# Loading the stacks of the RWKV chains in fourteen paced pieces instead of two bursts

## The chip, the cores and the metric

The kernel runs on one core of one Trainium2 chip. The metric is the device time of one launch in microseconds (us): the time before is the median of three runs. Beside those runs there is one profiled execution, from which every view of the profile is taken.

## The reference, cut to what matters

Two trunk layers work on 1024 latent and 256 context tokens of 1024 channels. Layer 0 mixes tokens with a bidirectional RWKV-7 recurrence, layer 1 with attention; both are followed by an MLP. The change lies inside the recurrence of layer 0, which for each of 16 heads of 64 channels, and for each of two directions, is

```
def _wkv_step(state, inp):
    r, w, k, v, kk, bvec = inp
    sa = jnp.einsum('bhvk,bhk->bhv', state, -kk)
    state = state * w[:, :, None, :] + sa[..., None] * bvec[:, :, None, :] + v[..., None] * k[:, :, None, :]
    y = jnp.einsum('bhvk,bhk->bhv', state, r)
    return state, y
```

`_rwkv_scans` runs it forward and backward, first over the context tokens (from a zero state) and then over the latent tokens (from the context's last state), and adds the two outputs.

## The kernel before

The recurrence is done in chunks of 32 tokens: 8 context chunks and 32 latent chunks, so 40 steps in a row. Per chunk the work is turned into small matrix products. An earlier stage (`Prep`) computes the operands and writes them to three DRAM tensors: `S["ST"]` (for every chunk the stationary operands of the first and last product, called the stack, and in its ninth slot the inverted triangular matrices), `S["LS"]` (the stationary operands of the state update) and `S["V"]` (the values).

The stage of the chains (`Chain`, `staggered`) then walks the 40 steps. Two neighbouring chunks form a granule; there are 20 granules, and the list `Chain.seq` gives their order. The 16 heads with their two directions are packed into four pairs (0 to 3); pairs 0 and 1 share one stack tile (`lp` 0), pairs 2 and 3 another (`lp` 1). One pair's step has four pieces of work, each with 16 small matrix products on TensorE:

- `ps_x` (L848): stack times the state and values in tile `SV`; ScalarE copies it to `X` (L850).
- `ps_x` (L854): the masked inverse `T` times `X`; the results are copied back into `SV` (L861). `T` for the next step is made by GpSimd (L830) from the ninth slot of the stack.
- `ps_s` (L868): `LS` times `SV`, the new state; VectorE scales it into the `SV` of the next step (L872).
- `ps_y` (L877): the second half of the stack times `SV`, the output, copied or added to `y` (L880, L882).

`staggered` counts ticks t: a step takes 16 ticks, a granule 32, and pair l does its four pieces at ticks 4l + 0, 5, 10 and 11 of each step. So four ticks hold one piece of each kind, of four different pairs, and TensorE always has other pairs' products between two dependent ones. The readout of finished blocks (`early`, `middle`) is woven between the ticks and runs mostly on VectorE and GpSimd.

The operands of granule i + 1 are loaded while granule i runs. The stack tiles have two buffers (pool `gp`), as have the `LS` and `SV` tiles, so a load of granule i + 1 waits until the readers of granule i - 1 are through. All loads are issued by SyncE, whose DMA queue (SP) works in order. `Chain.run` calls `load` at the start of pair 1's granule (tick 4, for `lp` 0) and of pair 3's granule (tick 12, for `lp` 1). One call issues the whole stack (1152 KB, L805), two `LS` transfers of 256 KB (L808) and, for `lp` 1, eight `SV` transfers of 64 KB (L811): 14 transfers and 3840 KB per granule, each waiting for its buffer only. The first granule's loads are issued ahead of the stage (`issue_after`).

The instructions are put on their engines by a scheduler that keeps the order of data; a hand-made dependency between two instructions can be added with `add_manual_dep`.

Of the kernel before, what the change touches and what calls it, by code (L numbers as in the profile page):

```python
# [9 lines left out]
F32 = mybir.dt.float32  # L10
# [19 lines left out]
QUAD = {(0, 0): 3, (0, 1): 1, (1, 0): 2, (1, 1): 0}  # L30
# [172 lines left out]
def drain(*gens):  # L203
    for g in gens:
        for _ in g:
            pass


def weave(main, n, *tracks):


    state = [[0, *t, *(0, n)[len(t) - 2:]] for t in tracks]
    for i, _ in enumerate(main):
        for t in state:
            while i >= t[3] and t[0] < t[1] * (i + 1 - t[3]) / (t[4] - t[3]):
                t[0] += 1
                next(t[2], None)
    drain(*(t[2] for t in state))


def _chain(gens):
    for g in gens:
        yield from g
# [551 lines left out]
class Lanes:  # L775
# [21 lines left out]
                nc.scalar.copy(t[rows, h].rearrange("p l d a e c -> p (l d a) e c"), eye)  # L797
        self.ST = {}

    def load(self, k, lp, i):  # L800

        nc, S = k.nc, k.S
        ST, LS, SV = self.gp.tile([128, 2, 9, 2, 64], F32, name="ST", tag=f"ST{lp}"), self.LS[lp][i % 2], self.SV[i % 2]
        self.ST[lp, i] = ST
        nc.sync.dma_start(out=ST.rearrange("p l u c e -> p (l u c e)"), in_=S["ST"][:, lp, i].rearrange("p l u c e -> p (l u c e)"))  # L805
        for h in range(2):
            anti = slice(64 - h * 64, 128 - h * 64)
            nc.sync.dma_start(out=LS[anti, h].rearrange("p l d a e c -> p (l d a e c)"), in_=S["LS"][h, i, :, :, lp * 2:lp * 2 + 2].rearrange("b s l d a f e -> (b s) (l d a f e)"))  # L808
        for a, h, d in itertools.product(range(2), range(2), range(2) if lp == 1 else ()):
            q = (QUAD[a, h] ^ 1) * 32  # L810
            nc.sync.dma_start(out=SV[q:q + 32, h, a, 2 * d:2 * d + 2].rearrange("p c l e -> p (c l e)"), in_=S["V"][a, h, :, Chain.seq[i][d]].rearrange("s c l e -> s (c l e)"))  # L811


class Chain:
# [17 lines left out]
    def step(self, s):  # L832
        k, nc, pr, L = self.k, self.k.nc, self.pr, self.L
        i, c = divmod(s, 2)
        both = lambda c: slice(c, 4 - c, 3 - 2 * c)
        gf, gb = self.seq[i]
        rev, lp, ln = gf > gb, pr // 2, pr % 2
        ST, ls, SV = L.ST[lp, i], L.LS[lp][i % 2], L.SV[i % 2]
        stack = lambda ct2, h, d, o: ST[:, ln, h * 4 + ct2 * 2 + d, c, o:o + 32]
        sv = lambda h, ct2, d: SV[:, h, ct2, 2 * d + (c ^ d), pr, :]  # L840
        units = [(ct2, h, d) for d in range(2) for ct2 in range(2) for h in range(2)]
        if s == 0:
            self.inverses(0)
        T = self.T
        xu = L.px.tile([128, 2, 2, 64], F32, name="ps_x", tag="xu")
        for ct2, h, d in units:
            q = QUAD[ct2, h] * 32
            nc.tensor.matmul(xu[q:q + 32, 0, d, :], stack(ct2, h, d, 0), sv(h, ct2, d), start=True, stop=True, tile_position=(0, q))  # L848
        X = L.xp.tile([128, 2, 64], F32, name="X", tag=f"X{pr}")
        L.copied = nc.scalar.copy(X, xu[:, 0])  # L850
        yield
        for ct2, h, d in units:
            q = QUAD[ct2, h] * 32
            nc.tensor.matmul(xu[q:q + 32, 1, d, :], T[:, d, q // 32, :], X[:, d, :], start=True, stop=True, tile_position=(0, q))  # L854
        lo, hi = sorted((2 * gf + c, 2 * gb + 1 - c))
        first = lo not in self.seen
        self.seen |= {lo, hi}
        for ct2 in range(2):
            for h in range(2):
                q = QUAD[ct2, h] * 32  # L860
                (nc.vector.tensor_copy if first and ct2 == h == 0 else nc.scalar.copy)(SV[q:q + 32, h, ct2, both(c), pr, :], xu[q:q + 32, 1])  # L861
        yield
        if s + 1 < self.n:
            self.inverses(s + 1)
            i2, c2 = divmod(s + 1, 2)
            pst = L.pss.tile([128, 2, 2, 64], F32, name="ps_s", tag="s")
            for ct2, h, d in units:
                nc.tensor.matmul(pst[h * 64:h * 64 + 64, ct2, d, :], ls[:, h, ln, d, ct2, :, c], sv(h, ct2, d), start=True, stop=True, tile_position=(0, h * 64))  # L868
            for h in range(2):
                rows = slice(h * 64, h * 64 + 64)  # L870
                pt = k.c["PT"][rows, pr * 2:pr * 2 + 2, :, s + 1].unsqueeze(3).to_broadcast([64, 2, 2, 64])
                nc.vector.tensor_tensor(L.SV[i2 % 2][rows, h, :, both(c2), pr, :], pst[rows], pt, ALU.mult)  # L872
        yield
        psy = L.py.tile([128, 2, 64], F32, name="ps_y", tag="y")
        for ct2, h, d in units:
            q = QUAD[ct2, h] * 32
            L.last = nc.tensor.matmul(psy[q:q + 32, d ^ rev, :], stack(ct2, h, d, 32), sv(h, ct2, d), start=True, stop=True, tile_position=(0, q))  # L877
        o = self.y[:, lo:hi + 1:hi - lo, :]
        if first:
            nc.scalar.copy(o, psy)  # L880
        else:
            nc.vector.tensor_tensor(o, o, psy, ALU.add)  # L882

    def run(self):
        for s in range(self.n):
            if self.pr % 2 and s % 2 == 0 and s // 2 + 1 < len(self.seq):
                self.L.load(self.k, self.pr // 2, s // 2 + 1)
            yield from self.step(s)
            yield

# [10 lines left out]


STAGES = (0, 5, 10, 11)


def staggered(gens):


    for t in range(16 * Chain.n + 16):
        for l, g in enumerate(gens):  # L910
            if t >= 4 * l and (t - 4 * l) % 16 in STAGES:
                next(g, None)
        yield


# [90 lines left out]
def phase_ab(k, xstack):  # L1006


    tc, nc, S = k.tc, k.nc, k.S
    with ExitStack() as es:  # L1010
# [4 lines left out]
        ips, rs, ws, ls, hs, ps = (ExitStack() for _ in range(6))  # L1015
# [17 lines left out]
        y = [yp.tile([128, 40, 64], F32, name=f"y{p}", tag=f"y{p}") for p in range(4)]  # L1033
        ro = [Readout(k, p, y[p], rn) for p in range(4)]

        def early():

            k.cload("lnq", pool=rn)
            k.tables = nc.scalar.preload_act_table_set("natural_log_exp_and_others")
            k.order(k.tables, L.copied)  # L1040
            yield from _chain([r.gates() for r in ro])
            for r in ro:
                yield from r.center(4, False)
                yield from r.scale(4, False)

        with ExitStack() as cs:
            L = Lanes(k, cs)
            with tc.issue_after(k.late.ins):
                for lp in range(2):
                    L.load(k, lp, 0)  # L1050
            middle = _chain([_chain([r.center(b, False), r.scale(b, False)]) for b in (1, 2) for r in ro])
            weave(staggered([Chain(k, L, p, y[p]).run() for p in range(4)]), 16 * Chain.n + 16, (4 * 4 + 4 * 7, early(), 16 * 5, 16 * 31), (8 * 7, middle, 16 * 33))
        ips.close()
        rs.close()
        xs = parts(xstack.enter_context(tc.tile_pool(name="xs", reuse_waits="tile", bufs=1, side="right")), range(KT))
# [35 lines left out]
        if k.dbg and "o" in k.O:  # L1091
            for ct in range(KT):
                for t0, n in TB:
                    t = tmp.tile([128, 512], F32, name="o_db", tag="ro_z")
# [353 lines left out]
def build(tc, I, O, dbg=None):  # L1448
    with ExitStack() as ctx:
        k = K(tc, I, O, ctx, dbg)  # L1450
        setup(k)
        with ExitStack() as xstack:
            xs, x, nm, xp = phase_ab(k, xstack)
            k.wp = [ctx.enter_context(tc.tile_pool(name=n, reuse_waits="tile", bufs=b)) for n, b in (("w1", 1), ("w2", 2))]
            ws = phase_c(k, xs, x, nm, xp)
            with ExitStack() as es:
                kp = es.enter_context(tc.tile_pool(name="kp", reuse_waits="tile", bufs=1))
                qp = es.enter_context(tc.tile_pool(name="qp0", reuse_waits="tile", bufs=1))
                mp = es.enter_context(tc.tile_pool(name="mp", reuse_waits="tile", bufs=2))
                qs = phase_d(k, ws, xs, kp, qp, mp)  # L1460
                xstack.close()
                xs = parts(xstack.enter_context(tc.tile_pool(name="xs1", reuse_waits="tile", bufs=1, side="right")), range(KT), NL)
                phase_e(k, xs, qs, qp, mp)
            phase_f(k, xs)
# [16 lines left out]
```

## Time and profile before

| | |
|---|---|
| median of three runs | 4084.34 us (4082.6 to 4092.13) |
| profiled execution | 4093.04 us |
| its span | 4091.3 us |
| mean granted TensorE clock over the span | 0.919 |
| TensorE matmul busy | 3611.4 us (88%) |
| TensorE weight load busy | 2802.6 us (69%) |
| VectorE / ScalarE / GpSimd busy | 2195.9 / 1512.4 / 1480.2 us |
| mean DMA rate over the span | 101 GB/s |
| stage of the chains | first product 1027.5 us, last product 1482.6 us after the span's start |

The profiled execution is one launch; its own time is 1.7 us over its span and 8.7 us over the median of the runs. In the views, PE is TensorE doing products, PEld its weight loads, DVE VectorE, ACT ScalarE, POOL GpSimd and SP SyncE. The page cuts the span into 40 slices and gives for each the busy share in tenths, the clock granted to TensorE and the use of the DMA engines; the stage of the chains fills slices 11 to 15. "Issue" as the reason of an idle time means that the engine waited for nothing that the profile shows.

### The profile page before, as it was taken

The numbers are of one execution on the slowest core, as the hardware profiler recorded it, in microseconds if no ns is written. First come the engines' busy times: TensorE is split into PE (matmuls) and PEld (weight loads), VectorE is DVE, ScalarE is ACT, GpSimd is POOL, SyncE is SP. The second block draws the span as 40 slices with busy tenths as digits, with TensorE's granted clock in tenths as the row PEclk, the third lists the DMA queues.
The fourth block names the chain that finished last, engine by engine and source line by source line (L and its number), as shares of the span: only waits on it lengthen the run. The fifth ranks groups of instructions, "written<-read, shape, count | busy, mean of one in ns | idle before, by whom it ended". The sixth has DMA issues, their size and how long they took to land.

```text
span 4091.3 us, 70381 instructions
## 1 busy us (share of the span) xinstructions
PE 3611.4 (88%) x28100; PEld 2802.6 (69%) x28100; DVE 2195.9 (54%) x3707; ACT 1512.4 (37%) x3223; POOL 1480.2 (36%) x1387
## 2 busy tenths in 40 slices
PE   5999766883666779999999999889999999999998
PEld 3667654663566558788888888675444477888886
DVE  6337789998544665533333334657666453333334
ACT  5765555453444443411111112433444422221122
POOL 3114775765332423211111111124787612222221
PEclk7999866885878789999999999999999999999999
DMA  7456777777666553311111111432110111111112
GB/s 280 145 195 165 167 175 172 164 169 198 164 171 184 155 146 85 126 42 39 37 42 37 37 37 60 150 89 88 32 32 16 57 42 47 47 44 49 52 52 67
DMA packets 380279, 414.73 MB, mean 101 GB/s; under 512 B 150944, under 2 KB 280224, under 8 KB 374704
## 3 DMA queue, kind: packets, MB, share of 16 engines
q1 hardware_dynamic: 378992, 408.93, 36.4%
q8 instruction: 221, 3.62, 0.4%
q0 software_dynamic: 960, 1.31, 0.2%
q14 instruction: 106, 0.87, 0.1%
HBM read 294.99 MB, written 117.11 MB: 101 GB/s over the span
## 4 chain that ended last, share of the span: by engine, by line
PE 64%; DVE 11%; issue 4%; DMA 4%; ACT 1%; POOL 1%; SPq 1%; DVEq 0%; POOLq 0%; ACTq 0%
PE ps_pj L271 44%; PE ps_av L1347 4%; PE ps_s L868 3%; PE ps_m L1224 2%; PE ps_s L1387 2%; PE ps_pj L290 2%; PE ps_s L1388 2%; PE ps_y L877 1%; DVE To L712 1%; DVE Tn L713 1%; PE ps_x L848 1%; PE ps_x L854 1%; DMA wmod<-in_wmod 1%; DVE sgw L630 1%; DVE KT L653 0%
## 5 line engine op out<-in xcount | busy, mean ns | idle before, releaser
L255 POOL TENSOR_TENSOR w_lo<-w_raw,w_hi 128x512 fp32r<-128x512 f32 (+1 forms) x292 | 478.9, 1641 | 1677.7 <-ACT w_hi L253 1657.6
L271 PE MATMUL ps_pj<-xh,w_hi 128*128 128x512 f32 (+1 forms) x1712 | 626.3, 367 | 5.2 <-ACT w_hi L253 4.9
L271 PE MATMUL ps_pj<-xh,w_lo 128*128 128x512 f32 (+1 forms) x1712 | 618.3, 365 | 7.1 <-POOL w_lo L255 7.0
L271 PE MATMUL ps_pj<-xl,w_hi 128*128 128x512 f32 (+1 forms) x1712 | 622.6, 364 | 0.0
L1105 DVE SCALAR_TENSOR_TENSOR xr<-ps_pj,c_mod,xr 128x512 f32<-128x512 f32 (+1 forms) x368 | 251.8, 686 | 567.0 <-PE ps_pj L271 566.2
L253 ACT CAST w_hi<-w_raw 128x512 fp32r<-128x512 f32 (+1 forms) x292 | 216.6, 742 | 826.0 <-PE ps_pj L271 618.5
L271 PE MATMUL ps_pj<-hid_l,w_hi 128*128 128x512 f32 (+1 forms) x1280 | 474.4, 371 | 0.0
L271 PE MATMUL ps_pj<-hid_h,w_hi 128*128 128x512 f32 (+1 forms) x1280 | 473.1, 371 | 0.0
L271 PE MATMUL ps_pj<-hid_h,w_lo 128*128 128x512 f32 (+1 forms) x1280 | 469.8, 370 | 0.0
L1129 DVE TENSOR_TENSOR m_q<-m_r 128x512 f32<-128x512 f32 x160 | 183.6, 1149 | 415.5 <-ACT m_r L1127 415.2
L271 PEld LDWEIGHTS ps_pj<-xh,w_hi 128*128 128x128 f32 x1712 | 324.7, 190 | 59.9 <-ACT w_hi L253 6.6
L271 PEld LDWEIGHTS ps_pj<-xh,w_lo 128*128 128x128 f32 x1712 | 322.8, 190 | 61.0 <-POOL w_lo L255 9.9
L271 PEld LDWEIGHTS ps_pj<-xl,w_hi 128*128 128x128 f32 x1712 | 324.4, 190 | 51.5 <-issue 1.4
L1398 POOL TENSOR_TENSOR acc<-acc,p 128x1024 f32<-128x1024 f32 x122 | 295.5, 2423 | 58.6 <-ACT p L1391 54.2
L271 PEld LDWEIGHTS ps_pj<-hid_h,w_hi 128*128 128x128 f32 x1280 | 241.4, 189 | 44.3
L271 PEld LDWEIGHTS ps_pj<-hid_h,w_lo 128*128 128x128 f32 x1280 | 241.1, 188 | 43.8
L271 PEld LDWEIGHTS ps_pj<-hid_l,w_hi 128*128 128x128 f32 x1280 | 241.4, 189 | 43.2
L1391 ACT ACTIVATE p<-ps_s 128x1024 f32<-128x1024 f32 x160 | 163.8, 1024 | 231.1 <-PE ps_s L1388 229.2
L271 PE MATMUL ps_pj<-xhi,w_hi 128*128 128x512 f32 (+1 forms) x576 | 228.6, 405 | 15.2 <-ACT xhi L479 9.6
L271 PE MATMUL ps_pj<-xlo,w_hi 128*128 128x512 f32 (+1 forms) x576 | 227.2, 395 | 8.3 <-DVE xlo L480 8.1
L1228 DVE TENSOR_REDUCE mc<-ps_m 128x1 f32<-128x512 f32 x256 | 174.7, 690 | 100.8 <-PE ps_m L1224 97.0
L271 PE MATMUL ps_pj<-xhi,w_lo 128*128 128x512 f32 (+1 forms) x576 | 222.4, 388 | 3.7 <-POOL w_lo L255 3.7
(236 smaller groups left out, 6813.9 us busy)
## 6 DMA issues: line engine op xcount, KB each, us to landing
ST<-d_ST SPq DMA_DIRECT2D x40, 1152.0 KB
wmod<-in_wmod SPq DMA_DIRECT2D x32, 1024.0 KB
w_raw<-in_m SPq DMA_DIRECT2D x64, 512.0 KB
w_raw<-in_m SPq DMA_DIRECT2D x128, 256.0 KB
d_ST<-AR SPq DMA_DIRECT2D x160, 128.0 KB
d_LS<-KT SPq DMA_DIRECT2D x320, 64.0 KB
d_ST<-G SPq DMA_DIRECT2D x160, 128.0 KB
LS<-d_LS SPq DMA_DIRECT2D x80, 256.0 KB
```

What stands on the lines that cost most here:

```text
L253: nc.scalar.copy(hi, raw)
L255: getattr(nc, eng).tensor_tensor(lo, raw, hi.bitcast(F32), ALU.subtract)
L271: i = nc.tensor.matmul(ps[:, :n], w[:, sl], x[:, t0:t0 + n], start=a, stop=z)
L290: nc.tensor.matmul(ps[:, :n], w[:, sl], x[:, t0:t0 + n], start=a, stop=z)
L868: nc.tensor.matmul(pst[h * 64:h * 64 + 64, ct2, d, :], ls[:, h, ln, d, ct2, :, c], sv(h, ct2, d), start=True, stop=True, tile_position=(0, ...
L1105: k.nc.vector.scalar_tensor_tensor(x[:, t0:t0 + n], ps[:, :n], g, x[:, t0:t0 + n], ALU.mult, ALU.add)
L1129: nc.vector.tensor_tensor(q[:, :n], r[:, :n], r[:, :n], ALU.mult)
L1224: line(nc.tensor.matmul(ps[:, o:o + n], Q[:, (t + i) * 128:(t + i) * 128 + 128], K_[:, t0:t0 + n], start=True, stop=True))
L1228: line(nc.vector.tensor_reduce(mc[:, t + u, t0 // 512:t0 // 512 + 1], ps, AX.X, ALU.max), "v")
L1347: line(nc.tensor.matmul(st["av"][e * 64:e * 64 + 64], k.V[:, kt, ct // 2 * 64:ct // 2 * 64 + 64], p[:, e], start=(kt == 0), stop=(kt == 9) ...
L1391: nc.scalar.activation(p, ps, AF.Exp)
L1398: (nc.vector if ct == KT - 1 and kt % 3 == 2 else nc.gpsimd).tensor_tensor(st["acc"], st["acc"], p, ALU.add)
```

## The change

`load` becomes a generator that sends the operands of both `lp` in fourteen pieces per granule. The stack of each `lp` goes in four transfers: for either pair the slots 4 to 8 (320 KB) and then the slots 0 to 3 (256 KB). Each `LS` transfer is a piece of its own, as before in size, and the eight `SV` transfers form two pieces of four, now behind `lp` 0 instead of `lp` 1. `staggered` starts the generator at the first tick of a granule and advances it at the ticks listed in `SENDS`. Every transfer gets a dependency on the product that was issued last at that tick (`L.mark`), so SyncE waits for that product before it issues the transfer. The first granule is loaded without such waits. `Chain.run` no longer calls `load`.

```
+SENDS = (2, 4, 6, 8, 9, 10, 12, 14, 16, 18, 20, 22, 23, 24)
...
+    def load(self, k, i, mark=None):
...
+        def send(out, src):
+            d = nc.sync.dma_start(out=out, in_=src)
+            if mark:
+                k.tc.add_manual_dep(d.ins, mark().ins.name, mybir.DependencyInfo(mybir.DependencyClass.Sync, mybir.DependencyReason.DATA), reason="pace")
+
+        SV = self.SV[i % 2]
+        for lp in range(2):
+            ST, LS = self.gp.tile([128, 2, 9, 2, 64], F32, name="ST", tag=f"ST{lp}"), self.LS[lp][i % 2]
+            self.ST[lp, i] = ST
+            for l, us in itertools.product(range(2), (slice(4, 9), slice(0, 4))):
+                send(ST[:, l, us].rearrange("p u c e -> p (u c e)"), S["ST"][:, lp, i, l, us].rearrange("p u c e -> p (u c e)"))
+                yield
+            for h in range(2):
+                anti = slice(64 - h * 64, 128 - h * 64)
+                send(LS[anti, h]..., S["LS"][h, i, :, :, lp * 2:lp * 2 + 2]...)
+                yield
+            for a in range(2) if lp == 0 else ():
+                for h, d in itertools.product(range(2), range(2)):
+                    q = (QUAD[a, h] ^ 1) * 32
+                    send(SV[q:q + 32, h, a, 2 * d:2 * d + 2]..., S["V"][a, h, :, Chain.seq[i][d]]...)
+                yield
...
     def run(self):
         for s in range(self.n):
-            if self.pr % 2 and s % 2 == 0 and s // 2 + 1 < len(self.seq):
-                self.L.load(self.k, self.pr // 2, s // 2 + 1)
             yield from self.step(s)
...
+    sends = iter(())
     for t in range(16 * Chain.n + 16):
+        i, at = divmod(t, 32)
+        if at == 0 and i + 1 < len(Chain.seq):
+            sends = L.load(k, i + 1, lambda: L.mark)
         for l, g in enumerate(gens):
             if t >= 4 * l and (t - 4 * l) % 16 in STAGES:
                 next(g, None)
+        if at in SENDS:
+            next(sends, None)
         yield
```

In `Chain.step` the four products set `L.mark` (`L.mark = nc.tensor.matmul(...)`), where before only the last one was kept, in `L.last`.

More of the change, by code (lines that the diff above doesn't have):

```diff
@@ L798, in __init__ @@
         self.ST = {}
-    def load(self, k, lp, i):
+    def load(self, k, i, mark=None):
         nc, S = k.nc, k.S
[L803 to L811, printed above, removed]
+        def send(out, src):
[11 more added lines that the diff above has]
+                anti = slice(64 - h * 64, 128 - h * 64)
+                send(LS[anti, h].rearrange("p l d a e c -> p (l d a e c)"), S["LS"][h, i, :, :, lp * 2:lp * 2 + 2].rearrange("b s l d a f e -> (b s) (l d a f e)"))
+                yield
+            for a in range(2) if lp == 0 else ():
+                for h, d in itertools.product(range(2), range(2)):
+                    q = (QUAD[a, h] ^ 1) * 32
+                    send(SV[q:q + 32, h, a, 2 * d:2 * d + 2].rearrange("p c l e -> p (c l e)"), S["V"][a, h, :, Chain.seq[i][d]].rearrange("s c l e -> s (c l e)"))
+                yield
 class Chain:
@@ L847, in step @@
             q = QUAD[ct2, h] * 32
-            nc.tensor.matmul(xu[q:q + 32, 0, d, :], stack(ct2, h, d, 0), sv(h, ct2, d), start=True, stop=True, tile_position=(0, q))
+            L.mark = nc.tensor.matmul(xu[q:q + 32, 0, d, :], stack(ct2, h, d, 0), sv(h, ct2, d), start=True, stop=True, tile_position=(0, q))
         X = L.xp.tile([128, 2, 64], F32, name="X", tag=f"X{pr}")
@@ L853, in step @@
             q = QUAD[ct2, h] * 32
-            nc.tensor.matmul(xu[q:q + 32, 1, d, :], T[:, d, q // 32, :], X[:, d, :], start=True, stop=True, tile_position=(0, q))
+            L.mark = nc.tensor.matmul(xu[q:q + 32, 1, d, :], T[:, d, q // 32, :], X[:, d, :], start=True, stop=True, tile_position=(0, q))
         lo, hi = sorted((2 * gf + c, 2 * gb + 1 - c))
@@ L867, in step @@
             for ct2, h, d in units:
-                nc.tensor.matmul(pst[h * 64:h * 64 + 64, ct2, d, :], ls[:, h, ln, d, ct2, :, c], sv(h, ct2, d), start=True, stop=True, tile_position=(0, h * 64))
+                L.mark = nc.tensor.matmul(pst[h * 64:h * 64 + 64, ct2, d, :], ls[:, h, ln, d, ct2, :, c], sv(h, ct2, d), start=True, stop=True, tile_position=(0, h * 64))
             for h in range(2):
@@ L876, in step @@
             q = QUAD[ct2, h] * 32
-            L.last = nc.tensor.matmul(psy[q:q + 32, d ^ rev, :], stack(ct2, h, d, 32), sv(h, ct2, d), start=True, stop=True, tile_position=(0, q))
+            L.mark = nc.tensor.matmul(psy[q:q + 32, d ^ rev, :], stack(ct2, h, d, 32), sv(h, ct2, d), start=True, stop=True, tile_position=(0, q))
         o = self.y[:, lo:hi + 1:hi - lo, :]
@@ L903, with staggered @@
 STAGES = (0, 5, 10, 11)
-def staggered(gens):
+SENDS = (2, 4, 6, 8, 9, 10, 12, 14, 16, 18, 20, 22, 23, 24)
+def staggered(k, L, gens):
+    sends = iter(())
     for t in range(16 * Chain.n + 16):
+        i, at = divmod(t, 32)
+        if at == 0 and i + 1 < len(Chain.seq):
+            sends = L.load(k, i + 1, lambda: L.mark)
         for l, g in enumerate(gens):
@@ L1048, in phase_ab @@
             with tc.issue_after(k.late.ins):
-                for lp in range(2):
-                    L.load(k, lp, 0)
+                drain(L.load(k, 0))
             middle = _chain([_chain([r.center(b, False), r.scale(b, False)]) for b in (1, 2) for r in ro])
-            weave(staggered([Chain(k, L, p, y[p]).run() for p in range(4)]), 16 * Chain.n + 16, (4 * 4 + 4 * 7, early(), 16 * 5, 16 * 31), (8 * 7, middle, 16 * 33))
+            weave(staggered(k, L, [Chain(k, L, p, y[p]).run() for p in range(4)]), 16 * Chain.n + 16, (4 * 4 + 4 * 7, early(), 16 * 5, 16 * 31), (8 * 7, middle, 16 * 33))
         ips.close()
```

## Prediction, made before the changed kernel ran

> **What bounds the kernel now.** I read the page first, for where the stage of the chains lies and what is full in it.
>
> ```profile
> span 4091.3 us, 70381 instructions
> PE 3611.4 (88%) x28100; PEld 2802.6 (69%) x28100; DVE 2195.9 (54%) x3707; ACT 1512.4 (37%) x3223; POOL 1480.2 (36%) x1387
> ...
> PE   5999766883666779999999999889999999999998
> ...
> PEclk7999866885878789999999999999999999999999
> DMA  7456777777666553311111111432110111111112
> ...
> q8 instruction: 221, 3.62, 0.4%
> ```
>
> Over the span PE is the bound, but slices 11 to 15 (counted from 1) have PE at 6 to 7 tenths with a lowered clock and DMA at 5 to 6: something else ends the waits there. The last line matters below: 221 packets of 3.62 MB, 16.4 KB each, on a queue for instructions. TensorE's 28100 products and 28100 weight loads over 221 make 254 instructions a packet.
>
> Then the busy time of the stage in stretches (us; PE, PEld, DVE, ACT, POOL with counts, granted clock, DMA share, GB/s).
>
> ```profile
> 1069.50:1117.30 47.80, 33.90 (x1138) 29.02 (x1138) 19.63 (x52) 23.04 (x88) 13.94 (x19) 0.82 0.68 181
> 1117.30:1139.00 21.70, 13.38 (x293) 11.76 (x294) 19.98 (x48) 6.92 (x31) 15.79 (x16) 0.61 0.61 156
> 1139.00:1385.00 246.00, 171.19 (x5692) 147.82 (x5692) 100.66 (x266) 111.38 (x448) 65.13 (x90) 0.81 0.66 179
> 1385.00:1438.00 53.00, 38.47 (x1005) 30.25 (x994) 48.10 (x113) 23.13 (x96) 39.31 (x41) 0.74 0.57 153
> 1438.00:1462.00 24.00, 15.01 (x462) 13.07 (x464) 8.21 (x23) 9.28 (x36) 5.11 (x7) 0.79 0.64 171
> ```
>
> In 1117 to 1139 and 1385 to 1438 VectorE is busy 20.0 of 21.7 and 48.1 of 53 us: the woven readout is the bound, and loads change nothing there. In 1069 to 1117, 1139 to 1385 and 1438 to 1462, together 317.8 us, no engine is full. What PE waits for there (us, times, longest):
>
> ```profile
> PE ps_y L877 <- issue: 28.2, 11, 4.8
> PE ps_x L848 <- issue: 26.1, 10, 4.7
> PE ps_s L868 <- issue: 22.2, 8, 4.5
> PE ps_x L854 <- issue: 20.7, 10, 4.7
> ```
>
> 97.2 us of "issue", spread over all four kinds of product: no data dependency looks like that. Cutting the stage at the ends of these idle times shows what they are; first two granules amid the loads, then three stretches in the last granule, which loads nothing.
>
> ```profile
> 1306.48:1313.43 6.95, 5.40 (x128) 4.58 (x128) 2.27 (x6) 2.59 (x10) 1.47 (x2) 0.62 0.82 214
> 1313.43:1327.62 14.19, 9.35 (x380) 7.91 (x380) 6.80 (x18) 7.70 (x30) 4.40 (x6) 0.92 0.61 167
> 1327.62:1334.57 6.95, 5.06 (x127) 4.32 (x127) 2.27 (x6) 2.59 (x10) 1.46 (x2) 0.66 0.85 240
> 1334.57:1350.08 15.51, 10.72 (x380) 9.32 (x381) 6.79 (x18) 7.70 (x30) 4.39 (x6) 0.87 0.57 157
> ...
> 1467.01:1471.02 4.01, 3.12 (x127) 2.69 (x127) 2.26 (x6) 2.59 (x10) 1.47 (x2) 1.00 0.03 6
> 1471.02:1474.75 3.73, 3.09 (x128) 2.64 (x128) 2.23 (x6) 2.59 (x10) 1.47 (x2) 1.00 0.02 4
> 1474.75:1478.89 4.14, 2.68 (x128) 2.34 (x128) 2.92 (x9) 2.59 (x10) 0.00 (x0) 1.00 0.01 4
> ```
>
> Every stretch holds 128 products and 128 weight loads, or three times that (380 with a few records missing): 256 instructions, one 16.4 KB packet. So PE stops at the edge of each block of instructions and waits for the next. I call that a page. A page takes 3.96 us (mean of the last three rows) with the DMA engines idle, where PE is busy 2.96 of it; amid a burst of loads it takes 6.95. A granule is 4 pages and takes (6.95 + 14.19 + 6.95 + 15.51) / 2 = 21.8 us; I use 21.9.
>
> Last, the burst: SP's issues, the chain of waits, and the packets by queue between 1298.7 and 1303.5 and from there to 1305.
>
> ```profile
> 1295.98 1.73 SPq L808 DMA_DIRECT2D LS<-d_LS  x2
> 1297.81 0.53 SPq L805 DMA_DIRECT2D ST<-d_ST  x1
> 1299.56 1.49 SPq L808 DMA_DIRECT2D LS<-d_LS  x2
> 1301.15 0.53 SPq L805 DMA_DIRECT2D ST<-d_ST  x1
> 1301.73 12.25 SPq L811 DMA_DIRECT2D SV<-d_V  x8
> ...
> 1301.77 4.71 issue
> ...
> q1 hardware_dynamic: 219, 1.40, 93.8%
> ...
> q8 instruction: 1, 0.02, 5.5%
> ```
>
> PE stops at 1301.77; up to 1303.5 only data moves, then the one instruction packet comes, and PE goes on at 1306.48. The page was asked for while a whole stack (1152 KB, issued 1297.81) was being moved.
>
> **The change part by part.** *Bytes.* None is added.
>
> ```profile
> DMA packets 18058, 68.41 MB, mean 173 GB/s; under 512 B 4904, under 2 KB 4904, under 8 KB 13621
> q1 hardware_dynamic: 17973, 67.15, 62.9%
> ```
>
> These rows are for 1066 to 1462 us: 67.15 MB in 396 x 0.629 = 249 us of full engines, 270 GB/s. A granule's 3840 KB (3.93 MB) take 14.6 us of the DMA engines, a whole stack 4.4, a 320 KB piece 1.2, a 256 KB piece 1.0. Stack rows shrink from 9216 to 2560 and 2048 bytes; nothing here shows stack rows of that length, so I bound the effect by 0 and a tenth (1.5 us a granule), and take 0: below 18 us per granule the DMA engines do not decide either way.
>
> *The wait for a page.* Now a page next to a burst is late by 6.95 - 3.96 = 3.0 us, and the other late one of a granule by 14.19 - 3 x 3.96 = 2.3 to 15.51 - 3 x 3.96 = 3.6 us: half to four fifths of a whole stack's 4.4 us, as if the page waits for the rest of the transfer under way. With pieces of 1.0 to 1.2 us the same share is 0.5 to 1.0 us; I take 0.75. Pieces go out at ticks 2 to 24 of 32, so about three to four pages of a granule meet one: 3.5 x 0.75 = 2.6. Granule: 4 x 3.96 + 2.6 = 18.4 us, 3.5 less than 21.9. Lowest: no page meets anything, 15.8, 6.1 less. Highest, if each of four pages waits a whole piece: 4 x (3.96 + 1.2) = 20.6, 1.3 less. There are 317.8 / 21.9 = 14.5 such granules: 51 us, with 19 and 88 as ends.
>
> Here the Trainium skill (DMA: Bandwidth & Descriptors, Queues, rings and completion order) says that each DMA engine takes turns between queues, but drains a whole packet of descriptors from one before it turns to the next. No view here shows packets' borders; the lateness of 2.3 to 3.6 us against a stack's 4.4 agrees with it, and by it the new lateness is at most one piece, the 20.6 above.
>
> *The clock.* It was 0.62 and 0.66 in the two pages after long stops, where PE is busy 5.40 and 5.06 us, and 1.00 in the last granule, whose stops are of 0.6 to 1.5 us (4.01 - 3.12, 4.14 - 2.68). I take it as 1.00, since the new stops are nearer to those: a page of 4.7 us then covers 2.96 us of products. If that cover goes and all pages run at 0.62 to 0.66, a granule is 4 x 5.2 = 20.8, 1.1 less than now: 16 us in all, the high end beside the 19 above.
>
> *SP's queue.* 20 transfers a granule instead of 14.
>
> ```profile
> L805 SPq DMA_DIRECT2D ST<-d_ST x40: 337/525/1415, 994.5 to 1447.6; - x40
> L808 SPq DMA_DIRECT2D LS<-d_LS x80: 444/538/1866, 1011.2 to 1446.9; - x80
> L811 SPq DMA_DIRECT2D SV<-d_V x160: 302/412/1340, 1013.9 to 1461.1; - x160
> ```
>
> 8 x 0.525 + 4 x 0.538 + 8 x 0.412 = 9.6 us of 18.4: it fits. Each transfer now waits for a product, and behind it in the queue stand only the later pieces, which want later products anyway. Is any late? A tick is 18.4 / 32 = 0.58 us. The first stack pieces go at ticks 2 to 8 and are needed by `T` at 26; `SV` at 12 and 14 for 32; the second stack from 16, needed by `T` from 34: at least 18 ticks, 10 us, against a burst's backlog now of some 15 us that arrives in time. Cost 0. All buffers are free at these ticks (the last readers of granule i - 1 are at tick 7). The products that transfers wait for may need a signalling instruction of their own on PE, which the trace prices here:
>
> ```profile
> L854 PEldq EVENT_SEMAPHORE  x160: 51/51/51, 1030.7 to 1479.6; - x160
> ```
>
> 19 x 14 of 0.051 us are 14 us at most; a product can signal by itself, so I take 0.
>
> *Start of the stage.* Granule 1's data end the wait at 1069.5:
>
> ```profile
> 1047.05 1.09 SPq L808 DMA_DIRECT2D LS<-d_LS  x2
> ...
> 1053.43 13.12 DMA ST<-d_ST
> 1066.57 2.90 DMA SV<-d_V
> ```
>
> `SV`, last in the burst, goes out before the second stack after the change. From 1041 a granule of 18.4 us would start the next at 1060; I take 8 us, with ends 0 and 15.
>
> *Sum.* 51 + 8 = 59 us off 4093.04 is 4034. The profiled execution lies 8.7 us over the median, 4084.34, so the median comes to 4025. Later stages only move forward.
>
> **Rivals.** *No change* (0.11): lateness is spread, not shortened: four pages late by 1.5 us each give 4 x (3.96 + 1.5) = 21.8, as now, near 4084. For it: the same 14.6 us of transfers meet the pages, and PE and transfers now pace each other. Against: each transfer is a quarter as long. The Trainium skill's page Runtime: NRT & Kernel Launch (Instruction fetch mechanics) also says that crossing a 16 KiB boundary is mostly hidden; by that the stops are something else, and the time would stay too, at 4084. The trace disagrees: the stops come at each 256th instruction, even at a DMA share of 0.02; this reading has 0.02 of the 0.11.
>
> *Slower* (0.16): a page waits for the queue, however short the piece. Then three of four pages, not two, are late by the present 3.0 us: 3 x 6.95 + 3.96 = 24.8, 2.9 more, 14.5 x 2.9 = 42 us: 4126. It decides from a late page of (21.9 - 3.96) / 3 = 6.0 us. For it: nothing in the trace shows a page beside a small stack piece. Against: the instruction packet came when the whole stack's move was nearly done. The skill's DMA page (Rules for kernel authors) also advises at least 1 MiB per DMA; by 270 GB/s alone nothing is lost.
>
> *Floor* (0.12): nearly no page is late, 15.8 us: 88 + 15 = 103 off, 3981.
>
> **How the numbers follow.** Forecast (granule 17 to 20 us; 3994 to 4062): 0.53. Floor (below 3994) 0.12. A gain, but less (4062 to 4072): 0.08. No change: 0.11. Slower: 0.16. A measurement of this kernel tells about 0.3%, 12 us, from no change: faster 0.73, same 0.11, slower 0.16. The 8 in 10 range leaves out the slower case and the last of the floor: 3978 to 4094; the forecast's own is 3994 to 4062.
>
> **What would show it.** In the changed profile: pages of 256 instructions of 4.4 to 5.2 us instead of 6.95; issue idle on PE in more, shorter pieces with a clock near 1.00; granules of 18 us with a DMA share near 0.8; the two VectorE-bound stretches as long as before. Wrong if pages stay near 7 us beside pieces, if PE waits for `ST` or `SV` to land, or if the readout stretches grow.

## The result, and the profile after

The changed kernel takes 4031.0 us (median of 4 runs, 4028.6 to 4039.2) against 4086.5 us before (median of 4 runs, the three from above and one more, 4082.6 to 4092.1): a ratio of 0.9876 with a 95% interval of 0.986 to 0.9893, 55.5 us less. The profiled executions are 63.6 us apart (4093.04 and 4029.49); the one before lies 6.5 us over its median, the one after 1.5 us under.

First the page of the changed kernel, for the same places as before.

```profile
span 4027.7 us, 70776 instructions
...
PE   5999866885677779999999999899999999999998
...
PEclk7999965886898789999999999999999999999999
...
q8 instruction: 222, 3.64, 0.4%
```

The stage of the chains is shorter by half a slice (448.9 us before and 397.7 after, from the first copy of `X` to the last), and it begins earlier; the instruction packets are one more, of the same size. To see where in the stage the time went I cut both kernels at the same pieces of work: granules 2 and 3, 4 (with readout), 5 to 15, 16 and 17 (with readout), and the rest up to the last copy of `X`. Before:

```profile
1069.91:1114.76 44.85, 31.10 (x1040) 26.77 (x1040) 18.05 (x48) 21.73 (x82) 11.39 (x16) 0.81 0.66 179
1114.76:1141.97 27.21, 18.86 (x518) 16.44 (x514) 23.72 (x57) 10.65 (x47) 19.82 (x21) 0.69 0.59 147
1141.97:1386.63 244.66, 169.85 (x5638) 146.64 (x5636) 99.93 (x263) 110.25 (x443) 64.37 (x88) 0.80 0.67 180
1386.63:1443.52 56.89, 39.62 (x1024) 31.41 (x1024) 48.36 (x115) 23.36 (x96) 39.31 (x41) 0.74 0.54 146
1443.52:1479.33 35.81, 25.89 (x961) 22.32 (x957) 17.87 (x49) 19.41 (x75) 9.51 (x13) 0.88 0.43 113
```

After:

```profile
1058.59:1096.03 37.44, 29.46 (x1037) 25.19 (x1026) 18.81 (x50) 21.68 (x82) 12.21 (x17) 0.86 0.79 220
1096.03:1122.41 26.38, 19.15 (x514) 16.46 (x512) 23.04 (x55) 10.65 (x48) 18.91 (x20) 0.74 0.55 159
1122.41:1323.84 201.43, 149.91 (x5632) 128.94 (x5628) 99.85 (x263) 107.65 (x441) 64.17 (x88) 0.92 0.75 215
1323.84:1383.10 59.26, 40.10 (x1029) 31.82 (x1028) 48.52 (x115) 23.30 (x97) 39.30 (x41) 0.71 0.56 151
1383.10:1413.89 30.79, 24.64 (x964) 21.03 (x952) 16.73 (x44) 19.25 (x75) 9.51 (x13) 0.94 0.48 134
```

Granules 5 to 15 are the cleanest measure, since no readout runs beside them: 244.66 / 11 = 22.24 us a granule before, 201.43 / 11 = 18.31 after. In the third row the products are the same and the work of VectorE, ScalarE and GpSimd is within 3%; the granted clock rises from 0.80 to 0.92 and the DMA share from 0.67 to 0.75, because the same bytes move in less time. The 65.4 us by which the last copy comes earlier are 43.2 from granules 5 to 15, 7.4 from 2 and 3, 5.0 from the last row, 0.8 from granule 4, less 2.4 in granules 16 and 17, and 11.3 from the start (granule 2 begins at 1058.59 instead of 1069.91). All the readout granules together are 1.5 us slower; VectorE is busy 48 us in 16 and 17 either way.

The 11.3 us of the start do not come from faster granules. The stage's first product is issued at 1013.2 us instead of 1027.5, because VectorE clears `SV` (L792), for which that product waits, at 1012.3 instead of 1026.5: the changed kernel has this ahead of some of `Prep`'s last work on VectorE, not behind it. Granules 0 and 1 themselves then take 42.40 us instead of 39.47. What in the change gave VectorE this other order isn't shown.

What PE waits for in granules 5 to 15, after (us, times, longest):

```profile
PE ps_s L881 <- issue: 19.8, 11, 2.5
PE ps_y L890 <- issue: 12.7, 9, 2.6
PE ps_x L867 <- issue: 9.2, 9, 2.0
PE ps_x L861 <- issue: 8.7, 6, 2.5
```

Still "issue", and still at the edges of 256 instructions: the longest stop is now 2.6 us where it was 4.8. In these granules the waits for "issue" add up to 50.4 us, where they were 74.3, and PE's busy time is 149.91 us, where it was 169.85 at the lower clock. Most pages end in such a stop in both kernels (30 stops over 0.15 us before and 36 after, in some 44 pages); there slower products only fill a wait. Cut at those edges, a stretch of the changed kernel reads:

```profile
1299.37:1303.41 4.04, 3.09 (x128) 2.69 (x127) 2.26 (x6) 2.57 (x10) 1.45 (x2) 1.00 0.43 117
1303.41:1308.46 5.05, 3.11 (x126) 2.66 (x126) 2.27 (x6) 2.59 (x11) 1.45 (x2) 1.00 1.00 293
1308.46:1316.39 7.93, 7.17 (x252) 6.29 (x252) 4.54 (x12) 4.14 (x16) 2.19 (x3) 0.78 0.77 222
1316.39:1320.63 4.24, 3.15 (x128) 2.62 (x127) 2.27 (x6) 2.58 (x10) 1.46 (x2) 1.00 0.64 168
```

A page takes 4.0 to 5.1 us here (two in the third row), even at a DMA share of 1.00, and 18.31 / 4.06 = 4.5 on average (1040 instructions, 16 of them for semaphores, are 4.06 pages); before, a page amid a burst took 6.95.

### The profile page after: what moved, and what is told of

The parts are those of the page before. It is cut to its first block, busy times and chain, and to the rows that moved or that the text cites. A ratio compares the mean times of both kernels' runs of the same rounds, so it can differ in the third digit from the quotient of the medians.

```text
span 4027.7 us, 70776 instructions
## 1 busy us (share of the span) xinstructions
PE 3598.4 (89%) x28100; PEld 2789.5 (69%) x28100; DVE 2199.1 (55%) x3707; ACT 1507.4 (37%) x3223; POOL 1478.4 (37%) x1387
## 4 chain that ended last, share of the span: by engine, by line
PE 66%; DVE 11%; issue 4%; DMA 2%; ACT 1%; POOL 1%; SPq 1%; DVEq 0%; POOLq 0%; ACTq 0%
PE ps_pj L271 45%; PE ps_av L1364 4%; PE ps_s L881 2%; PE ps_m L1241 2%; PE ps_s L1404 2%; PE ps_pj L290 2%; PE ps_s L1405 2%; DVE Tn L713 1%; DVE To L712 1%; PE ps_y L890 1%; PE ps_x L861 1%; PE ps_x L867 1%; DVE sgw L630 1%; DVE KT L653 0%; DVE AR L647 0%
```

## Experiments

The number that I compare is the time of a granule, granules 5 to 15 in each kernel's own profile: 22.24 before, 18.31 after. Each run's row shows the length of those eleven granules first and the clock, the DMA share and GB/s last. The time of the whole launch says less about the loads: the first copy of `X` comes at 1030 us before, at 1016 after and anywhere from 1010 to 1026 in the runs below.

### Is it the fetch of instructions? No loads, and more instructions

No loads from granule 2 on:

```
-        if at == 0 and i + 1 < len(Chain.seq):
+        if i and at == 0:
+            for lp in range(2):
+                L.ST[lp, i + 1] = L.ST[lp, (i + 1) % 2]
+        elif at == 0:
             sends = L.load(k, i + 1, lambda: L.mark)
```

> The changed kernel without the loads of granules 2 to 19, which work on the operands of granules 0 and 1 again (this part of the computation is left out). If pages of instructions are late only through the loads: 16.0 us a granule (4 pages of 3.96 us and ten instructions), a granted clock of 1.00, stops of 0.6 to 1 us at every 256th instruction, about 3990 us in all. If the stops have another cause: 18.3 us a granule as with the loads.

More instructions for the same columns, again without loads:

```
-            L.mark = nc.tensor.matmul(psy[q:q + 32, d ^ rev, :], stack(ct2, h, d, 32), sv(h, ct2, d), ...)
+            for o in (0, 32):
+                L.mark = nc.tensor.matmul(psy[q:q + 32, d ^ rev, o:o + 32], stack(ct2, h, d, 32), sv(h, ct2, d)[:, o:o + 32], ...)
```

> As the run without loads, but each ps_y product is made as two of 32 columns each: the same columns in all, 32 more instructions in each 128 of a pair's step, five pages a granule instead of four. The operands of granules 2 to 19 are left out again. If the fetch of instructions sets the pace: 5 x 3.96 = 19.8 us a granule, about 4060 us. If the array or the data set it: PE's work grows by at most the ps_y weight loads (0.27 us in 1.44), which its idle time covers, 16 to 17 us a granule, about 3995 us.

The eleven granules of the first and, below, of the second:

```profile
1115.65:1276.13 160.48, 137.93 (x5640) 117.56 (x5632) 100.72 (x266) 108.62 (x443) 64.65 (x89) 1.00 0.02 5
```

```profile
1122.73:1326.66 203.93, 149.70 (x7053) 128.58 (x7042) 100.87 (x267) 110.67 (x442) 64.97 (x89) 1.00 0.02 5
```

Without loads a granule takes 14.59 us (3969 us in one run), 1.4 less than I expected. PE still stops; the waits of that run:

```profile
PE ps_y L890 <- issue: 7.8, 15, 0.9
PE ps_s L881 <- issue: 6.0, 12, 0.8
PE ps_x L867 <- issue: 5.7, 11, 0.8
```

With the few stops that this view puts down to other engines these are 43 of 0.3 to 0.9 us, one at every 127th product: with as many weight loads and two instructions for semaphores that makes 256. With a quarter more instructions a granule takes 18.54 us (4032 us in one run), 27% more and between the two expectations (19.8, and 16 to 17), while the busy time of TensorE's products and weight loads rises only by 9%, no other engine's by more than 2%, the clock is full and the DMA engines are idle. The waits of the second run show what fills the difference:

```profile
PE ps_y L891 <- issue: 15.4, 21, 1.2
PE ps_x L867 <- issue: 14.1, 11, 1.7
PE ps_x L861 <- issue: 11.4, 11, 1.5
PE ps_s L881 <- issue: 10.6, 10, 1.3
```

51.5 us of short stops, and none of the long ones. So the stage goes at the pace of the instruction pages even with nothing else on the DMA engines, 14.59 / 4.03 = 3.62 us a page (1032 instructions, 8 of them for semaphores, are 4.03 pages) and 18.54 / 5.03 = 3.69 with the quarter more, though such a page holds less work. Loads add 7.65 us a granule before, 3.72 after.

The packets of the instruction queue in the traces tell what such a page is made of. In the run without loads, for instance, PE resumes at 1121.91, the next packet moves from 1123.06 to 1124.01, and PE, stopped again since 1125.02, resumes at 1125.35. In the eleven granules of that run the packet starts 1.2 us on average (1.05 to 1.73) after the stop that began the page, takes 1.1 us, and PE resumes 1.4 us after its end, 3.7 in all. So it looks as if a page is asked for only when the one before it begins; none of these packets starts earlier. Beside the loads the last two parts hardly change (1.2 and 1.5 us before, 1.1 and 1.4 after). The first grows, to 3.2 us on average and 6.5 at most before, 1.95 and 3.1 after: the lateness lies in the wait until the packet starts.

### Size and pacing, one at a time

Pieces without waits (`sends = L.load(k, i + 1)`, so `mark` is None):

> The changed kernel with its fourteen pieces, but without the waits: the transfers are issued in the same order as soon as their buffers are free. A granule (eleven of them without a readout) takes 22.2 us before and 18.3 us after the change. Theory A (a page of instructions waits for the transfer that is under way, so the size of a piece decides): 18 to 19 us a granule, 4030 to 4040 us in all. Theory B (a page waits for all that is queued, so the pacing decides): the burst is whole again, 21 to 22 us a granule, 4075 to 4090 us.

Whole stacks with waits:

```
-            for l, us in itertools.product(range(2), (slice(4, 9), slice(0, 4))):
-                send(ST[:, l, us]..., S["ST"][:, lp, i, l, us]...)
-                yield
+            send(ST..., S["ST"][:, lp, i]...)
+            yield
...
+SENDS = (2, 9, 10, 12, 14, 16, 23, 24)
```

> The changed kernel with its waits, but each stack in one transfer of 1152 KB (at ticks 2 and 16); LS and SV go at their ticks as after the change. Theory A (size decides): two pages a granule meet a whole stack, 20.5 to 22 us a granule, 4060 to 4085 us. Theory B (pacing decides): 18.3 to 19.5 us a granule, 4030 to 4045 us.

The first, then the second:

```profile
1133.72:1340.26 206.54, 149.46 (x5638) 129.03 (x5635) 99.97 (x263) 107.05 (x443) 64.37 (x88) 0.93 0.74 213
```

```profile
1127.51:1335.34 207.83, 158.88 (x5638) 136.71 (x5636) 100.46 (x266) 108.96 (x442) 63.17 (x87) 0.87 0.69 212
```

Pieces alone: 18.78 us a granule, ratio 0.9915 (0.9898 to 0.9931). For the granule that is what the theory that size decides said, and against the rival. Whole stacks with waits: 18.89 us, ratio 0.9922 (0.9901 to 0.9942), which is what the rival said, and against mine. In all the two take 4047 and 4050 us, over the 4030 to 4040 and 4030 to 4045 that went with those granules. Each half of the change alone brings most of the 3.9 us a granule; together they bring 18.31. Both theories fall in their strict form.

What the two have in common, and the kernel before has not, is the order: `SV` behind the first stack. So I took both halves away and left the order (whole stacks, `mark` None):

> The changed kernel's order (SV before the second stack), but whole stacks and no waits: only the order differs from the kernel before. So far a granule takes 22.2 us before, 18.3 after, 18.8 with pieces and no wait, 18.9 with whole stacks and waits, 14.6 without loads. Theory C (a page that is asked for while a stack moves waits for the rest of that move, and in a burst this happens for both stacks; either small pieces or a gap between the stacks cures it): 21.5 to 22.5 us a granule, 4065 to 4085 us. Theory D (what the kernels with 18.3 to 18.9 have in common, SV between the stacks, is the cure): 18.5 to 19.5 us, 4040 to 4055 us.

```profile
1138.13:1369.00 230.87, 161.87 (x5637) 140.15 (x5632) 101.33 (x268) 108.41 (x441) 65.46 (x90) 0.84 0.64 191
```

20.99 us a granule, ratio 0.9966 (0.9952 to 0.9981): between the two expectations for the granule. The order, with the later issue of some transfers, is worth 1.25 us of the 3.93; pieces take it 2.2 further, waits 2.1.

Then the waits with other ticks only, `SENDS = (8, 9, 10, 11, 12, 13, 14, 15)`:

> Whole stacks, each transfer behind a product as in the run with whole stacks and waits, but at the ticks 8 to 15 one after the other, so the two stacks follow each other again with LS and SV between. Theory C (the gap between the stacks is the cure when they are whole): 20.5 to 22.3 us a granule, 4060 to 4085 us. If to wait for a product is itself the cure: 18.5 to 19.3 us, 4040 to 4055 us.

```profile
1136.24:1368.66 232.42, 164.54 (x5639) 142.05 (x5636) 100.00 (x263) 109.73 (x442) 62.99 (x87) 0.82 0.63 190
```

21.13 us, within theory C's range, and 4087 us in one run, just over it. Same transfers, same order, each behind a product: so it is not the wait as such that helps but the ticks. SP's issues show the difference; clumped, then spread:

```profile
1205.22 0.34 SPq L805 DMA_DIRECT2D ST<-d_ST  x1
...
1208.08 6.15 SPq L805 DMA_DIRECT2D SV<-d_V  x8
1214.98 0.34 SPq L805 DMA_DIRECT2D ST<-d_ST  x1
1215.42 1.09 SPq L805 DMA_DIRECT2D LS<-d_LS  x2
1227.99 0.34 SPq L805 DMA_DIRECT2D ST<-d_ST  x1
```

```profile
1206.60 0.34 SPq L805 DMA_DIRECT2D ST<-d_ST  x1
...
1210.90 6.61 SPq L805 DMA_DIRECT2D SV<-d_V  x8
1217.62 0.36 SPq L805 DMA_DIRECT2D ST<-d_ST  x1
1219.27 1.09 SPq L805 DMA_DIRECT2D LS<-d_LS  x2
1223.52 0.34 SPq L805 DMA_DIRECT2D ST<-d_ST  x1
```

Clumped, SP issues nothing for 11.5 us after 1216.5; spread, for 3.2 us. The run with the order alone isn't spread either: after one `LS` transfer SP stands still for 7 us, until products have read the next one's buffer (`1208.59 9.47 SPq L805 DMA_DIRECT2D LS<-d_LS  x3` in its queue). So with whole stacks the slow granules go with a long pause and loads close together; that this is the cause is argued from three runs, not shown. That the distance between the two stacks is what counts (theory C's reason) is not borne out: it is 9.8 us in the clumped run and 11.0 in the spread one.

### Bytes of a transfer or length of its rows

The quarter pieces also have shorter rows (2560 and 2048 bytes instead of 9216). Three runs without waits take the two apart. Pieces of 32 partitions with whole rows, `for r in range(0, 128, 32): send(ST[r:r + 32]...)`:

> As the run with pieces and no wait, but each stack is cut into four pieces of 32 partitions with whole rows of 9216 bytes (288 KB each) instead of pieces of all partitions with rows of 2560 and 2048 bytes. If the bytes of a transfer decide (theory C): 18.3 to 19.5 us a granule, 4035 to 4055 us. If the length of a row decides: 21 to 22.5 us, 4065 to 4090 us.

Two pieces to a stack by pair, `for l in range(2): send(ST[:, l]...)`:

> As the run with pieces and no wait, but two pieces of 576 KB to a stack (rows of 4608 bytes) instead of four. Theory C: between whole stacks and quarters, 19.5 to 21 us a granule, 4050 to 4070 us. Theory D (the order is the cure): 18.5 to 19.3 us, 4040 to 4050 us.

Two pieces by slots over both pairs, `for us in (slice(4, 9), slice(0, 4)): send(ST[:, :, us]...)`:

> As the run with two pieces to a stack and no wait (576 KB each, rows of 4608 bytes, 20.5 us a granule), but the two pieces are cut by slots over both pairs: 640 and 512 KB, rows of 2560 and 2048 bytes, as short as those of the four pieces (18.8 us a granule without waits). If the bytes of a transfer decide how late a page is: 20 to 21 us a granule, 4055 to 4070 us. If the length of its rows decides: 18.4 to 19.3 us, 4035 to 4050 us.

In the order of the three:

```profile
1139.86:1388.91 249.05, 170.93 (x5638) 148.03 (x5633) 99.97 (x262) 109.96 (x441) 63.94 (x88) 0.82 0.79 177
```

```profile
1137.36:1363.02 225.66, 162.47 (x5638) 140.61 (x5636) 101.41 (x268) 108.28 (x442) 65.40 (x90) 0.85 0.66 195
```

```profile
1138.09:1364.08 225.99, 160.27 (x5637) 138.62 (x5636) 100.48 (x266) 108.64 (x443) 64.28 (x89) 0.86 0.68 195
```

The pieces of 32 partitions give 22.64 us (4096 us in one run), a little over what was expected if rows decide; but with them a granule's loads also move more slowly, 177 / 0.79 = 224 GB/s of full engines against 213 / 0.74 = 288 with the other quarters, so this run proves nothing on rows. It does show that a small transfer alone is no cure. The two halves settle the rows: 4608 bytes 20.51 us (4066 us in one run), 2560 and 2048 bytes 20.54 us (ratio 0.9957, 0.994 to 0.9974). Between these two the length of the rows makes no difference; over all partitions the size of a transfer, or their number, does: 20.5 with halves, 18.78 with quarters. The step from wholes (20.99) to halves is some 5 us over the eleven granules, less than what single runs with wholes differ by (4065 to 4083 us), and so not shown. Why halves help so little and quarters so much is open.

### Further along the same way

Twice as many pieces (stack pieces by slots 6 to 8, 4 and 5, 0 and 1, 2 and 3; `LS` by pair; `SV` by two; `SENDS = tuple(range(1, 29))`):

> The changed kernel with 28 pieces a granule, one at each of the ticks 1 to 28: stack pieces of 192 and 128 KB with rows of 1536 and 1024 bytes, LS pieces of 128 KB with rows of 2048, SV in four pieces of two transfers. If shorter pieces and rows make pages less late: 16.8 to 18.0 us a granule, 4005 to 4027 us. If SyncE becomes the limit (32 transfers a granule of about 0.5 us are 16 us of its time, beside the waits), or nothing is left to gain: 18.2 to 19.5 us, 4030 to 4050 us.

```profile
1124.80:1342.69 217.89, 163.82 (x5648) 135.83 (x5639) 102.86 (x272) 107.78 (x441) 62.65 (x87) 0.91 0.66 197
```

19.81 us a granule, ratio 0.9919 (0.9904 to 0.9933): slower than fourteen pieces, and than either expectation allowed. SP's issues and then the waits of PE and of GpSimd say why:

```profile
1200.16 3.68 SPq L805 DMA_DIRECT2D ST<-d_ST  x8
1203.94 3.22 SPq L805 DMA_DIRECT2D LS<-d_LS  x4
1207.27 5.50 SPq L805 DMA_DIRECT2D ST<-d_ST  x8
1212.85 2.37 SPq L805 DMA_DIRECT2D LS<-d_LS  x4
1215.31 4.69 SPq L805 DMA_DIRECT2D SV<-d_V  x8
```

```profile
PE ps_x L863 <- DMA SV<-d_V: 19.1, 20, 2.7
PE ps_s L883 <- issue: 9.5, 7, 2.0
PE ps_x L863 <- issue: 8.8, 6, 2.0
PE ps_x L869 <- issue: 8.6, 10, 1.5
```

```profile
POOL T L845 <- DMA ST<-d_ST: 64.3, 15, 9.1
```

"Issue" on PE falls from 50.4 to 27.5 us (0.6 of them in a stop not shown), but SyncE issues without a pause, the data come late, and PE waits for `SV` and `T` for the stack. That the pages are less late doesn't follow: a page can arrive while PE waits for data. PE's idle waits add up to 52 us in either kernel; what is longer is the busy time of the product that waits for `SV` (L863), 54.1 us for 42.3, probably because its products now come one by one as their operands land.

The same fourteen pieces spread evenly, `SENDS = (1, 3, 5, 7, 9, 11, 13, 15, 17, 19, 22, 25, 28, 31)`:

> The changed kernel with its fourteen pieces at the ticks 1, 3, 5, 7, 9, 11, 13, 15, 17, 19, 22, 25, 28, 31 instead of 2 to 24. If what remains of the lateness comes from pieces that queue up behind each other: 17.3 to 18.0 us a granule, 4012 to 4027 us. If each page meets the piece under way whatever the spacing: 18.1 to 18.6 us, 4028 to 4036 us.

```profile
1126.56:1326.53 199.97, 154.83 (x5630) 133.36 (x5627) 99.93 (x263) 108.70 (x443) 63.92 (x88) 0.90 0.77 218
```

18.18 us a granule, 4029.9 us, ratio 0.9864 (0.9849 to 0.9879): not to be told from the changed kernel's 18.31 us and 4031.0, as the second expectation said.

## Why the prediction was right, and where it was not

The forecast was 4025 us, the result 4031.0; in the profiles 59 us off against 63.6.

- *The bound.* Right, and now shown: a stop at every 256th instruction, without loads too, and time in proportion to the number of instructions. The 97.2 us of "issue" were those of the whole stretch from 1069 to 1462, the two readout stretches with them; in granules 5 to 15 they are 74.3.
- *The granule.* 18.4 forecast, 18.31 measured, but by two errors that cancel, which is luck. The free page was taken as 3.96 us from three pages of the last granule; it is 3.62. The lateness was taken as 2.6 us a granule; it is 18.31 - 14.59 = 3.72. Three to four pages late by 0.75 us were forecast; it is all four, by 0.9 on average, and the pages shown take 0.4 to 1.4 us over the free one. 1.4 is more than the 1.2 that a whole 320 KB piece takes by the prediction's own rate, so the bound of one piece does not hold for every page.
- *The reason.* Half right. That a page waits for the rest of the one transfer under way made size the only cure. The runs show two: pieces without waits 18.78, whole stacks spread by waits 18.89. How a spread of whole stacks helps as much isn't settled: in the run with the new order alone (20.99), stacks were issued 9 to 11 us apart too.
- *Count.* 14.5 granules at 3.5 us, 51 us forecast; granules 2, 3 and 5 to 15 and the last row brought 55.7.
- *Start.* 8 us forecast, 11.3 measured, and this too is luck. The reason given, that granule 1 waits for `SV`, was not in the trace: PE waits there for 0.2 us (`PE ps_x L848 <- DMA SV<-d_V: 0.2, 1, 0.2`). Granules 0 and 1 took 2.9 us longer, and the gain came from a stage that began 14.3 us earlier, of which the prediction says nothing. Take that off, and 49 of the 63.6 us between the profiles are left.
- *Readout.* Taken as untouched; 1.5 us slower in all.
- *Clock.* Taken as 1.00, it was 0.92 in granules 5 to 15, up from 0.80. What that cost was not measured by itself; most pages still end in a stop, and there slower products only shorten the stop.
- *SP.* Right for fourteen pieces (20 transfers): in granules 5 to 15 no wait of PE for `ST` or `SV` is listed, though GpSimd's `T` waits 13.1 us for the stack. The run with 28 pieces shows where that ends: 32 transfers of some half a microsecond in a granule below 20 us.
- *Range.* Its bounds of 3994 and 4062 are not what granules of 17 and 20 us give with the prediction's own terms: 14.5 x 4.9 + 15 = 86 and 14.5 x 1.9 = 28 us off, 3998 to 4057. The result lies in either.
- *Rivals.* Slower would have needed three late pages of 6.0 us in a granule; a page takes 4.5 on average. No change is refuted. With the Trainium skill's statement (Runtime: NRT & Kernel Launch, Instruction fetch mechanics) that the crossing of a 16 KiB boundary is mostly hidden the trace agrees only in part: without loads PE is busy for 3.1 of a page's 3.6 us and stops for 0.3 to 0.9, but more instructions still take more time in proportion, and beside whole stacks stops reached 4.8. The Trainium skill's 1 MiB per DMA (DMA: Bandwidth & Descriptors, Rules for kernel authors) is given there for bandwidth and was the wrong guide for this stage: with wholes and no waits a granule takes 20.99 us, with pieces of 320 and 256 KB 18.78. The floor was set too high: it is 14.59 us a granule, not 15.8.

## What to carry to other kernels

When TensorE idles for "issue" at a fixed count of instructions, suspect its instruction stream: count the products and weight loads between two stops, and divide all of them by the packets of the instruction queue; here both gave some 256. Loads that are hidden behind the work can then still cost time, because an instruction packet starts later beside them (1.2 us after its page began without loads, 3.2 before the change). Cut them to a few hundred KB over all partitions or spread them over the work; either brought most of the gain here, while pieces of 288 KB to 32 partitions brought none. Stop before the issuing engine is full: at 32 transfers a granule data came late, and 1.5 of the 3.9 us were lost again. The number of instructions weighs as much as the loads: without loads, a quarter more cost 3.95 us a granule, as much as the whole change brought. Whether fewer would save as much was not tried.

## What the runs showed of the hardware

- TensorE's instructions, with small products, came at one page of 256 in 3.62 us with idle DMA engines; 5/4 of the instructions took 18.54 / 14.59 = 1.27 of the time.
- Of a page without loads, 1.2 us pass before its successor's packet starts, 1.1 us while it moves and 1.4 us from its end until TensorE goes on (means of one run). Beside unpaced whole stacks (before) only the first part grew much, to 3.2 us on average.
- With the stacks sent to 32 partitions at a time, a granule's loads moved at 224 GB/s of full DMA engines, with quarter pieces over 128 partitions at 288.
- The granted clock was lower where the stops were longer: over eleven granules 0.80 to 0.87 in the seven kernels with stops of 3.2 us and more, 0.90 to 0.93 in the four whose longest waits were 2.6 to 3.1, and 1.00 in the two without loads, with stops up to 0.9 and 1.7.
